# Where the columns of the convolution input and of the gates are computed: whole at the seams, or a few products at a time inside scans and inverses

## The chip, the core and the metric

The kernel runs on one core of a Trainium2 chip. The metric is the device time of one execution in microseconds. The kernel before takes 3205.15 us, the median of three runs (3204.31 to 3208.82).

## What is computed

A decoder trunk of two layers over 528 tokens (16 learned ones put ahead of 512) of width 1024. A layer is a half-step SwiGLU feed-forward, a mixer of two parallel branches, and a second half-step feed-forward; after each comes a layer norm of the sum with what went in. The mixer, cut to what matters here:

```python
z = x @ w_in
glu_a, glu_b, zr, gate_c, gate_r = split(z)          # 1024, 1024, 3328, 1024, 1024 columns
u  = glu_a * sigmoid(glu_b)
yc = silu(layer_norm(conv31(u) + conv_b)) @ conv_wo  # causal, 31 taps, a filter for each channel
yr = rwkv7(zr) @ rwkv_wo                             # 16 heads of 64, a recurrence over the tokens
h  = sigmoid(gate_c) * yc + sigmoid(gate_r) * yr
out = h @ w_out
```

The recurrence keeps a 64 x 64 state S for each head, and each token does `S = S*w + (S @ -kk) (kk*a) + v k`, then `y = S @ r`.

## The kernel before

Everything is float32 in and out. Channels lie on the 128 partitions, tokens along the free axis. A large product is made of three: each operand is split into a high and a low part of a faster 32-bit format (`split`, `wunit`: ACT copies the high part of a weight block, DVE subtracts it from the raw block to get the low one), and high x high, high x low and low x high are added up in PSUM. A **column** is a block of 128 output channels of `x @ w_in`: 8 blocks of 128 input channels x 3 parts x 2 halves of the tokens (264 each) = 48 matmuls of one line (`mac`, L214). Its weights, 512 KB, come by one DMA from SP's queue (L117), and `w_raw` has two buffers. Its result is a PSUM tile `mm`, of which there are two; ACT or DVE reads it out.

The mixer of one layer has these columns: two for the low-rank inputs of the recurrence and one for the first part of the convolution's gate (computed at the mixer's start); three for each of the eight pairs of heads (`prep_pair`: key, receptance, value); and the **31 columns that this change is about**, which stand with one step that needs no column of its own in the list `fill`: `glu_b` and `glu_a` for each of the eight blocks of the convolution's input (after `glu_a` the block's 31 taps can run on DVE, `taps`, L872), then 16 `gate`s. A `gate` column goes through ACT (L884) and a DMA to memory, where the mixer's end fetches it.

The recurrence is done in chunks of 64 tokens, for four **quarters** of four heads each, one after the other. For a quarter q:

- `prep(q)`: six columns and their elementwise work on ACT and DVE.
- `scores(q)`: for each of eight chunks the products of keys and receptances (L1034, L1043), copied by ACT and masked by DVE. They use the one PSUM tile `sc`. Scores of q + 1 are issued in the steps of scan q.
- `substitution(q, g)`: the diagonal 16 x 16 blocks of half g of the chunks are inverted by thirty small DVE instructions; the inverses go through memory into `dd` (L1086, L1089, SP's queue).
- `inverse(q, g)`: for 16 matrices of 64 x 64 at a time, PE joins those blocks: a first round of matmuls (L1112), a mask on DVE (L1113), then three rounds (L1121) with ACT copies (L1125) between them. A fp32 matmul stands as two in the trace.
- `meta(q)`: the 16 learned tokens.
- `scan(q)`: eight **steps**, one for each chunk. In a step PE transposes v (L1183), ACT copies it twice (L1184, L1186), PE multiplies by the state (L1188), ACT copies (L1190), PE applies the inverse (L1196) and reads the state (L1198), ACT copies (L1201), PE updates the state (L1205), DVE adds and scales it (L1208, L1209), and PE finishes the output (L1213), which ACT copies (L1218).
- `post(q)`: a group norm, transposes (L1303), and the result to memory, in the steps of the next scan; for the last quarter in the steps of its own scan and behind it.

The stretch between two scans, with `substitution(q + 1, 1)`, `inverse(q + 1, 0)`, `meta(q + 1)` and `prep(q + 2)`, is called a **seam** below. `inverse(q, 1)` is issued behind step 0 of scan q.

The order of the instructions on each engine is made when the program is built: a planner walks through time by a model of the instructions' durations, and on each engine takes the ready instruction that stands earliest in the program. So program order is priority: work that stands later is drawn forward to where an engine would wait, as far as its inputs and buffers allow. On the chip each engine runs its queue strictly in that order. `high_priority(offset=-n)` makes scores (50) and taps (150) stand later than they are written.

Where columns of `fill` stand in the program is a table of counts: `START` and `LOWSTEP` in the low-rank part, `FILL0` for the chunks of the first scores, `FILLP` inside `prep`, `FILL` behind the steps of each scan, `FILLS` at the seams, and `LAST`, the number kept for the very end, behind the transposes of the last group norm (`self.later = self.turned`). The call is always for whole columns: `filler(n)` pops n entries and each computes all of its 48 products at that place. Before, 8 entries go in the low-rank part, 4 in the first scores, 2 in `prep(1)`, 3 at the first seam, 1 in `prep(2)`, 3 at the second seam, 4 at the third, 3 behind steps of scan 3, 2 after it, then the rest.

## Time and profile before

| | |
|---|---|
| median of three runs | 3205.15 us (3204.31 to 3208.82) |
| the profiled execution: its time, its span | 3213.03 us, 3211.3 us |
| mean granted TensorE clock in it | 0.971 |
| PE, DVE, ACT busy | 3129.7, 1893.0, 1224.3 us |
| HBM read and written | 270.81 MB, 47.12 MB |

The span lies within the profiled execution's own time; the profiled execution was a little longer than the timed runs. "PE" is TensorE's matmuls and "PEld" its weight loads; a matmul's duration includes the depth of the pipeline, so successive matmuls overlap in the record and the starts tell the rate. In a timeline a row is a start, the time from the first start to the last end of a merged group, engine, line, operation, what is written and read, and how many; what follows in brackets is idle time before it and who ended it. In windows a row is a stretch, its length, busy time and count of each engine, the granted clock, the share of the DMA engines and GB/s. The four scans of layer 0 lie between 622 and 1050 us of the span, those of layer 1 between 2232 and 2643.

### The profile page before, as it was taken

What the parts mean: (1) busy time and instruction counts of PE and PEld (TensorE: products, weight loads), DVE (VectorE), ACT (ScalarE), POOL (GpSimd) and SP (SyncE); (2) the same over time, 40 slices, a digit from 0 to 9 for tenths busy, and PEclk for the clock granted to TensorE, in tenths of its full rate; (3) what the DMA queues carried; (4) which work ended last, traced back from release to release, by engine and by line L of the source; (5) the groups of instructions that cost most, each with busy time, mean ns of one, the idle gap of its engine ahead of it and who ended that gap; (6) DMA issues with size and microseconds to landing.
All of it is one profiled execution on the core that took longest, in us unless ns stands there. A gap on an engine that the chain in (4) does not pass through costs nothing.

```text
span 3211.3 us, 64489 instructions
## 1 busy us (share of the span) xinstructions
PE 3129.7 (97%) x27172; PEld 3006.6 (94%) x27172; DVE 1893.0 (59%) x3827; ACT 1224.3 (38%) x2271; POOL 24.0 (1%) x95
## 2 busy tenths in 40 slices
PE   9999999999999899999999999899999999999998
PEld 8999989988889899999989999899899889999997
DVE  4343377886786766343463434777887758653435
ACT  4232254343454534232242322543444445242322
POOL 0000000000000000000000000000000000000000
PEclk9999999997999999999999999998999999999998
DMA  5232244332333552232232322343333325432321
GB/s 153 74 109 83 76 137 149 93 81 77 92 104 92 172 150 80 79 108 81 79 96 74 111 80 81 130 143 91 82 92 104 107 82 179 119 106 77 115 72 54
DMA packets 569776, 326.45 MB, mean 102 GB/s; under 512 B 84940, under 2 KB 536896, under 8 KB 569486
## 3 DMA queue, kind: packets, MB, share of 16 engines
q1 hardware_dynamic: 563374, 308.49, 33.6%
q10 hardware_dynamic: 4608, 8.52, 0.7%
q0 software_dynamic: 1504, 5.33, 0.5%
q8 instruction: 213, 3.49, 0.4%
q14 instruction: 77, 0.63, 0.1%
HBM read 270.81 MB, written 47.12 MB: 99 GB/s over the span
## 4 chain that ended last, share of the span: by engine, by line
PE 89%; DVE 5%; ACT 3%; DMA 2%; issue 1%; SPq 0%; ACTq 0%; POOL 0%; POOLq 0%; DVEq 0%
PE mm L196 54%; PE mm L214 19%; PE sc L1121 3%; PE sc L1043 1%; PE tr L1188 1%; PE ch L1213 1%; PE tr L1196 1%; PE ch L1205 1%; PE sc L1112 1%; PE sc L928 1%; PE sc L797 1%; PE tr L1183 1%; DVE w_lo L139 1%; DVE ln_rstd L390 1%; PE sc L1034 1%
## 5 line engine op out<-in xcount | busy, mean ns | idle before, releaser
L196 PE MATMUL mm<-xh,w_hi 128*128 128x264 f32 (+1 forms) x2880 | 818.9, 285 | 17.6 <-ACT xh L404 16.6
L196 PE MATMUL mm<-xh,w_lo 128*128 128x264 f32 (+1 forms) x2880 | 820.2, 285 | 0.5 <-DVE w_lo L139 0.5
L196 PE MATMUL mm<-xl,w_hi 128*128 128x264 f32 (+1 forms) x2880 | 818.1, 284 | 0.3 <-DVE xl L405 0.2
L139 DVE TENSOR_TENSOR w_lo<-w_raw,w_hi 128x1024 fp32r<-128x1024 f32 (+3 forms) x520 | 528.7, 1017 | 438.8 <-ACT w_hi L128 418.9
L128 ACT CAST w_hi<-w_raw 128x1024 fp32r<-128x1024 f32 (+2 forms) x400 | 385.3, 964 | 765.7 <-PE mm L196 522.0
L196 PEld LDWEIGHTS mm<-xh,w_hi 128*128 128x128 f32 x2880 | 545.1, 190 | 20.7 <-ACT xh L404 18.2
L196 PEld LDWEIGHTS mm<-xh,w_lo 128*128 128x128 f32 x2880 | 546.3, 190 | 0.8 <-DVE w_lo L139 0.8
L196 PEld LDWEIGHTS mm<-xl,w_hi 128*128 128x128 f32 x2880 | 545.6, 189 | 1.4 <-DVE xl L405 1.3
L196 PE MATMUL mm<-hl,w_hi 128*128 128x264 f32 (+1 forms) x1408 | 400.5, 284 | 0.0
L196 PE MATMUL mm<-hh,w_hi 128*128 128x264 f32 (+1 forms) x1408 | 400.4, 284 | 0.0
L196 PE MATMUL mm<-hh,w_lo 128*128 128x264 f32 (+1 forms) x1408 | 398.7, 283 | 0.0
L214 PE MATMUL mm<-xh,w_hi 128*128 128x264 f32 x1760 | 393.6, 300 | 1.7 <-DVE tmp L747 1.7
L214 PE MATMUL mm<-xh,w_lo 128*128 128x264 f32 x1760 | 392.4, 299 | 0.3 <-DVE w_lo L139 0.3
L214 PE MATMUL mm<-xl,w_hi 128*128 128x264 f32 x1760 | 386.4, 297 | 0.0
L872 DVE SCALAR_TENSOR_TENSOR cacc<-cu,cw,cacc 128x528 f32<-128x528 f32 (+1 forms) x480 | 355.1, 751 | 5.9 <-ACT cacc L870 2.7
L214 PEld LDWEIGHTS mm<-xh,w_hi 128*128 128x128 f32 x1760 | 287.6, 195 | 9.2 <-DVE tmp L747 2.2
L214 PEld LDWEIGHTS mm<-xh,w_lo 128*128 128x128 f32 x1760 | 286.6, 195 | 7.3 <-DVE w_lo L139 0.7
L214 PEld LDWEIGHTS mm<-xl,w_hi 128*128 128x128 f32 x1760 | 285.5, 195 | 6.3
L452 DVE TENSOR_TENSOR g<-g,mm 128x264 f32<-128x264 f32 (+1 forms) x176 | 74.6, 427 | 329.3 <-PE mm L196 318.5
L196 PEld LDWEIGHTS mm<-hh,w_lo 128*128 128x128 f32 x1408 | 265.1, 188 | 0.1
L196 PEld LDWEIGHTS mm<-hl,w_hi 128*128 128x128 f32 x1408 | 265.0, 188 | 0.2
L196 PEld LDWEIGHTS mm<-hh,w_hi 128*128 128x128 f32 x1408 | 264.6, 188 | 0.1
(312 smaller groups left out, 4381.3 us busy)
## 6 DMA issues: line engine op xcount, KB each, us to landing
w_raw<-in_w_in_dram SPq DMA_DIRECT2D x116, 512.0 KB
w_raw<-in_ffn_wg_dram SPq DMA_DIRECT2D x88, 512.0 KB
w_raw<-in_ffn_wu_dram SPq DMA_DIRECT2D x88, 512.0 KB
w_raw<-in_ffn_wd_dram SPq DMA_DIRECT2D x64, 384.0 KB
w_raw<-in_ffn_wd_dram SPq DMA_DIRECT2D x64, 320.0 KB
w_raw<-in_rwkv_wo_dram SPq DMA_DIRECT2D x16, 512.0 KB
w_raw<-in_conv_wo_dram SPq DMA_DIRECT2D x16, 512.0 KB
w_raw<-in_w_out_dram SPq DMA_DIRECT2D x16, 512.0 KB
```

The costliest lines, as they stand in the source:

```text
L128: copy = self.nc.scalar.copy(hi[:, :kt], raw[:, :kt])
L139: sub = self.nc.vector.tensor_tensor(lo[:, k], raw[:, k], hi[:, k].bitcast(F32), op=ALU.subtract)
L196: self.nc.tensor.matmul(pm, a[:, k, :], b[:, xk + k, s], start=first and k == 0 and j == 0, stop=last and k == nk - 1 and j == 2)
L214: m = nc.tensor.matmul(pm[:, h, :n], a[:, wk + k, :], b[:, xk + k, s:s + n], start=first and k == 0 and j == 0, stop=last and k == nk - 1 ...
L390: nc.vector.reciprocal(rstd[:, :n], rstd[:, :n])
L452: nc.vector.tensor_tensor(g, g, ps[1][:, :n], op=ALU.mult)
L797: nc.tensor.matmul(pm, w[a][r, o, :], x[b][r, s], start=j == 0, stop=j == 2)
L872: tap = nc.vector.scalar_tensor_tensor(y, x, w, y, op0=ALU.mult, op1=ALU.add)
L928: nc.tensor.matmul(tr[:, 32 * j:32 * j + 32], sq[:, k0:k0 + P], self.bones[:, ::4], start=True, stop=True)
L1034: nc.tensor.transpose(ps[:, 0, 256 + p * P:256 + (p + 1) * P], FB[p][:, fs], self.ident)
L1043: pairs.append(nc.tensor.matmul(ps[:, e, p * P:(p + 1) * P], FB[p][r, fs], G[r, p, 1, :, cs], start=True, stop=True))
L1121: nc.tensor.matmul(ps[0:W, i, c0:C], vt[:, i, :], x[:, c0:C], start=True, stop=True)
```

## The change

`mac` becomes a generator, `macs`, that issues one product at a time. A new function, `pump(n)`, issues up to n products of the column that is open; when none is open it takes the next entry of `fill`, as long as a **quota** for this part of the program lasts, loads its weights if they aren't loaded, and orders the next entry's weights too if the quota goes on. A column's read-out follows its last product. `pump()` without a number finishes the open column and opens none.

A step of a scan calls it at four places: behind the copies of v, 4 products; behind the copy L1190, 5; behind the copy L1201, 4; at the end of the step's products, 7. An inverse calls it with 2 behind every fourth matrix, in the first round and in each of the three others. The quotas are 1 column for `inverse(0, 0)`, 4, 4, 4 and 3 for the four scans with the `inverse(q, 1)` in them, and 1 for each later `inverse(q + 1, 0)`. At the end of a scan the open column is finished and what is left of the quota is computed as whole columns.

The tables `FILL`, `FILLS` and `FILLP` are gone, so no whole columns of `fill` stand at the seams, in `prep` or behind steps; the first scores have 3 instead of 4, and `LAST` is 2 instead of 1. What the columns compute, their number and their order in `fill` stay.

```diff
-FILL0 = (0, 0, 0, 0, 2, 0, 0, 0, 2)
-FILL = ((0, 0, 0, 0, 0, 0, 0, 0), (0, 0, 0, 0, 0, 0, 0, 0), (0, 0, 0, 0, 0, 0, 0, 0), (0, 1, 0, 1, 0, 1, 0, 0))
-FILLS = (3, 3, 4, 2)
-FILLP = ((0, 0, 0, 0, 0, 0), (0, 0, 0, 0, 0, 2), (0, 0, 0, 0, 0, 1), (0, 0, 0, 0, 0, 0))
-LAST = 1
+FILL0 = (0, 0, 0, 0, 1, 0, 0, 0, 2)
+QUOTA0 = 1
+QUOTA = (4, 4, 4, 3)
+QUOTAI = (1, 1, 1)
+PUMP = (4, 5, 4, 7)
+PUMPI = 2
+LAST = 2
...
+    def macs(self, pm, w, x, t0, n, nk):
...
+                    yield m
...
         def prep(q):
             Q = {}
-            for i, _ in enumerate(self.prep(q, Q)):
-                filler(FILLP[q][i])
+            for _ in self.prep(q, Q):
                 self.taps(TAPP[q])
...
         self.substitution(0, 1, Q)
+        self.quota = QUOTA0
         self.inverse(0, 0, Q)
+        self.pump()
         self.meta(0, Q)
...
+            self.quota = QUOTA[q]
             for c, _ in enumerate(self.scan(q, Q)):
...
-                filler(FILL[q][c])
                 self.taps(TAP[q][c])
+            self.pump()
+            filler(self.quota)
             for _ in post:
                 pass
             if q < 3:
                 self.substitution(q + 1, 1, N)
+                self.quota = QUOTAI[q]
                 self.inverse(q + 1, 0, N)
+                self.pump()
                 self.meta(q + 1, N)
             post = early or self.post(q, Q)
-            filler(FILLS[q])
             Q, N = N, prep(q + 2) if q < 2 else None
...
+    def pump(self, n=None):
+
+
+        while n is None or n > 0:
+            if self.open is None:
+                if n is None or not self.quota or not self.fill:
+                    return
+                self.quota -= 1
+                col, done = self.fill.pop(0)
+                w = self.loaded.pop(col) if col in self.loaded else self.load_in(col)
+                if self.quota and self.fill:
+                    nxt = self.fill[0][0]
+                    self.loaded[nxt] = self.load_in(nxt)
+                pm = self.mm()
+                self.open = self.macs(pm, w, self.x, 0, T // 2, KT), done, pm
+            gen, done, pm = self.open
+            if next(gen, None) is None:
+                done(pm)
+                self.open = None
+            elif n is not None:
+                n -= 1
...
         for i in range(N):
             nc.tensor.matmul(ps[0:C, i, 0:W], U[:, i, :], d[:, i, 0:W], start=True, stop=True)
+            if i % 4 == 3:
+                self.pump(PUMPI)
...
                 nc.tensor.matmul(ps[0:W, i, c0:C], vt[:, i, :], x[:, c0:C],
                                  start=True, stop=True)
+                if i % 4 == 3:
+                    self.pump(PUMPI)
...
             nc.scalar.copy(va[0:C], hc(tr[0:C, 0:256]))
+            self.pump(PUMP[0])
...
             nc.scalar.copy(w[0:C], hc(tr[0:C, 256:512]))
+            self.pump(PUMP[1])
...
             nc.scalar.copy(va[C:P], hc(tr[C:P, 256:512]))
+            self.pump(PUMP[2])
...
+            self.pump(PUMP[3])
             ro = C * (c % 2)
```

More of the change, by code (lines that the diff above doesn't have):

```diff
@@ L212, in mac @@
                 for h in range(2):
-                    s = t0 + h * n
-                    m = nc.tensor.matmul(
-                        pm[:, h, :n], a[:, wk + k, :], b[:, xk + k, s:s + n],
-                        start=first and k == 0 and j == 0,
-                        stop=last and k == nk - 1 and j == 2)
+                    m = self.nc.tensor.matmul(
+                        pm[:, h, :n], a[:, k, :], b[:, k, t0 + h * n:t0 + (h + 1) * n],
+                        start=k == 0 and j == 0, stop=k == nk - 1 and j == 2)
                     if self.later is not None:
@@ L274, in setup @@
         self.first = None
+        self.later = None
     def fetch_x(self, h, room):
```

32 lines of the change are left out of this document (16 added, 16 removed).

## The prediction

> **What bounds the kernel now.** I read the page first: the shares by engine, then the chain that ended last.
>
> ```profile
> span 3211.3 us, 64489 instructions
> PE 3129.7 (97%) x27172; PEld 3006.6 (94%) x27172; DVE 1893.0 (59%) x3827; ACT 1224.3 (38%) x2271; POOL 24.0 (1%) x95
> PE 89%; DVE 5%; ACT 3%; DMA 2%; issue 1%; SPq 0%; ACTq 0%; POOL 0%; POOLq 0%; DVEq 0%
> ```
>
> TensorE bounds it: busy for 97% of the span and 89% of the chain. But a busy PE need not be a PE at full rate, so the second view is the windows, by stretch: the whole of each layer's mixer, beside 200 us of a feed-forward layer, and the same mixers for the column products alone (L214, the line this change hands out differently).
>
> ```profile
> 200.00:400.00 200.00, 200.00 (x1644) 199.83 (x1643) 74.58 (x119) 53.02 (x87) 0.00 (x0) 1.00 0.30 87
> 436.00:1072.00 636.00, 621.62 (x5921) 567.71 (x5922) 485.61 (x1166) 287.03 (x598) 8.57 (x36) 0.94 0.39 110
> 2036.00:2665.00 629.00, 615.32 (x5878) 563.25 (x5877) 471.57 (x1098) 286.35 (x593) 8.92 (x39) 0.95 0.39 112
> 436.00:1072.00 636.00, 384.34 (x2640) 345.13 (x2640) 0.94 0.39 110
> ```
>
> Columns here: stretch, its length, then busy time and count of PE, PEld, DVE, ACT, POOL (of PE and PEld alone in the last row), the granted clock, DMA share, GB/s. In the feed-forward a matmul starts every 200/1644 = 0.122 us at clock 1.00. A mixer has 2640 column products, 55 columns of 48, worth 321 us at that rate; its other 3281 matmuls, all smaller, and its waits fill the other half. And the mean clock is 0.94 and 0.95. Where it falls, it falls to 0.50, so (1 - 0.94) x 2 x 636 + (1 - 0.95) x 2 x 629 = 76 + 63 = 139 us of the mixers run at half clock. So what can be gained is in the scans and inverses: waits, and half-clock time. The total of the products is the same before and after.
>
> **The scans' steps.** Four windows that hold exactly six steps each (48 L1188 matmuls, eight a step), with the products in them:
>
> ```profile
> 662.00:698.00 36.00, 13.88 (x67) 9.62 (x68) 1.00 0.20 50
> 2273.00:2307.00 34.00, 12.18 (x58) 8.28 (x58) 1.00 0.21 52
> 2397.00:2437.00 40.00, 16.26 (x83) 11.51 (x83) 1.00 0.37 102
> 2515.00:2553.00 38.00, 14.33 (x68) 9.77 (x68) 1.00 0.36 98
> ...
> 662.00:698.00 36.00, 4.07 (x48) 3.24 (x48) 1.00 0.20 50
> 2515.00:2553.00 38.00, 4.03 (x48) 3.25 (x48) 1.00 0.36 98
> ```
>
> 148 us for 24 steps is 6.17 us a step, with 276/24 = 11.5 products in it already: columns of the seams are drawn into the steps today. The clock is 1.00. What a step costs without them is read off the starts in the timeline of PE, behind one row of the groups by line:
>
> ```profile
> L1196 PE MATMUL tr<-w,G 64*64 64x64 f32 x512 | 46.0, 232 | 0.5 <-ACT w L1190 0.5
> ...
> 689.63 0.68 PE L1205 MATMUL ch<-va,sb 128*64 128x64 f32 x8
> 690.25 0.41 PE L1183 MATMUL tr<-ident,v 128*64 128x128 f32 x2
> 690.58 0.71 PE L1043 MATMUL sc<-G,FB 64*128 64x128 f32 x8
> 691.23 0.68 PE L1213 MATMUL ch<-va,sb 128*64 128x64 f32 x8
> 691.84 0.39 PE L214 MATMUL mm<-xh,w_hi 128*128 128x264 f32 x1
> 692.06 0.41 PE L214 MATMUL mm<-xl,w_hi 128*128 128x264 f32 x2
> 692.31 0.29 PE L214 MATMUL mm<-xh,w_lo 128*128 128x264 f32 x1
> 692.52 0.68 PE L1188 MATMUL tr<-sv,G 128*64 128x64 f32 x8
> 693.13 0.39 PE L214 MATMUL mm<-xh,w_lo 128*128 128x264 f32 x1
> ```
>
> From start to next start L1205 and L1183 take 0.62 and 0.33 us, the scores' L1043 0.65, L1213 and L1188 0.61 each. L1196 runs side by side with L1198; its 46.0 us in 64 steps are 0.72 a step with the last one's tail, against 0.68 for the rows of eight here, so I take 0.61 for it too. The scores' two transposes I put at 0.2, from L1183's two at 0.33 less the change of shape. Together 3.63 us. The 11.5 products add 1.40. Another price shows: the last product before L1188 holds PE for 0.21 us where 0.122 is its rate. Going over to another weight shape costs 0.09, and about as much on the way back (inside the 0.61), so a run of products costs 0.2 us beside its length; four ways in add 0.36 a step. That leaves 6.17 - 3.63 - 1.40 - 0.36 = 0.78 us of true wait per step.
>
> After the change a step hands out 4 + 5 + 4 + 7 = 20 products, each group right behind a stage whose copy the chain waits for. With no wait left a step takes 3.63 + 20 x 0.122 + 0.36 = 6.43 us; with the waits as they are, 7.2. The 8.5 further products are worth 1.04 us elsewhere. So a step gains between 0 and 0.78 us; I take half of the wait as filled, 0.4 us. 24 steps of scans 0 to 2 and 112/20 = 5.6 of scan 3 are fed, 59 in both layers: **-24 us** (0 to -46). DVE hides the work that comes with it:
>
> ```profile
> 662.00:698.00 36.00, 35.97 (x408) 29.37 (x407) 30.48 (x57) 18.80 (x54) 0.00 (x0) 1.00 0.20 50
> L139 DVE TENSOR_TENSOR w_lo<-w_raw,w_hi 128x512 fp32r<-128x512 f32 x120 | 81.8, 682 | 14.1 <-ACT w_hi L126 9.1 <-PE mm L214 3.6 <-ACT w L1190 0.4
> ```
>
> DVE is at 30.48/36 = 85%. A column brings two L139 of 0.68 us: 8.5/48 of it a step is 0.24 us, on 5.1 us of DVE in a step of 6.8. It fits, since the convolution's taps give way. If it did not, L1208 would start late and the step lose that 0.24 us, 14 us in all. The weight loads are the same number, moved from the seams into SP's queue between the scores' stores; DMA is at 0.20 to 0.37 there, and each column is loaded one column ahead, so I cost that at nothing.
>
> The Trainium skill, page "TensorEngine Tiling (Array Packing)", section "Key Properties", says that changing the tiling mode, not just the tile, drains the TensorE; it speaks against short runs of products. The trace shows such a cost, 0.09 us a way, and by the rule it is paid at every switch. It changes a term of mine only where a switch is new, which is the next part.
>
> **The inverses.** The chain of waits at a seam shows how one runs today:
>
> ```profile
> 716.84 2.03 PE sc L1112 x32
> 718.88 4.15 PE mm L214 x20
> 723.03 1.56 PE sc L1121 x32
> 725.14 0.80 PE mm L214 x5
> 725.94 1.55 PE sc L1121 x32
> 728.56 0.80 PE mm L214 x5
> 730.65 2.69 PE sc L1121 x32
> ```
>
> Already 30 products lie in its waits, in three runs. The change puts two behind every four matrices, 16 places. I expect the first round's four places to be new runs and most later products to be drawn into the waits as now: four new pairs, 0.8 us, for 16 inverses 13 us; in the half that lies within a scan the PE changes shape anyway, so **+10 us** (+3 for one pair each to +42 for thirteen).
>
> The same rows show the half clock: 20 products took 4.15 us, 0.2 each, and the last round 2.69 us against 1.55. One inverse had almost no products to fill it (layer 0, scan 1):
>
> ```profile
> 772.00:806.00 34.00, 31.30 (x315) 26.50 (x314) 21.75 (x52) 14.21 (x36) 0.15 (x2) 0.65 0.14 41
> 772.00:806.00 34.00, 4.58 (x21) 3.09 (x20) 0.65 0.14 41
> ```
>
> 21 products in 34 us, and 0.35 x 2 x 34 = 24 us at half clock. The change hands out 32 in that inverse and 20 in each of its four steps, 112. The 91 more are worth 11 us; half of them in waits is **-6 us**. Of the 139 us at half clock I let a third go, 46 us; PE-bound work takes twice as long there, so at most 23 us, and with PE waiting part of it, **-14 us** (+10 if the seams lose as much as the inverses win; -50 if most of it goes).
>
> **What is left bare.** Two places lose their cover. At the seam before scan 3 no preparation of a next quarter follows. Today, in the 14 us from the end of scan 2 to the inverse:
>
> ```profile
> 962.00:976.00 14.00, 13.09 (x100) 12.39 (x100) 1.00 0.56 137
> 971.29 3.90 SPq L1089 DMA_DIRECT2D dd<-xdscr  x8
> ```
>
> 100 products fill the time until the diagonal blocks land (L1089). Afterwards the quota there is one column: 48. 52 x 0.122 = 6.3 us a layer lie idle, less some 1 us because longer steps of scan 2 let the blocks come in earlier: **+11 us** for both (0 to +16). The last group norm:
>
> ```profile
> 2646.55 0.41 PE L214 MATMUL mm<-xh,w_lo 128*128 128x264 f32 x2
> 2650.67 0.41 PE L1303 MATMUL tr<-ident,b 128*128 128x128 f32 x2 [3.71 <-DVE b L1262]
> ...
> 2658.28 0.40 PE L214 MATMUL mm<-xh,w_lo 128*128 128x264 f32 x2
> 2662.58 1.01 PE L196 MATMUL mm<-rh,w_hi 128*128 128x256 f32 x3 [3.89 <-ACT rh L103]
> ```
>
> Today one column is kept for behind the norm's transposes and PE idles 3.71 us before and 3.89 us after it. Keeping two fills the second gap, but nothing is left for before: the norm's 7 us lie bare, and the clock will be down when the two columns start. **+3 us** for both (-4 to +8).
>
> **The sum**: -24 + 10 - 6 - 14 + 11 + 3 = -20 us, made against the profiled execution's 3213.0 us (1.7 us around the span). That execution is 7.9 us above the median of the three times, 3205.15, and I carry the difference over: **3185 us**, 0.6% faster. A difference under 0.2%, 6.4 us, can't be told from none.
>
> **The rivals.** *Filled already* (3205): the steps hold 11.5 products today, and if the 0.8 us is the chain's own latency on ACT and DVE that more products only push back, each step lengthens by what it takes in, the switches take back what the clock gives, and -20 shrinks to within 6 us. For it: the window with 83 products took 40 us and that with 58 took 34; 6 us for 25 products is 0.24 each, twice the rate, if nothing else differs (scores and transposes do).
>
> *Bare seams* (3229, slower): the columns are used up in the steps and PE waits at the seams. If the prepared columns don't cover seams 0 and 1 either, because their evictions wait on DVE behind the substitution, then three columns less there leave some 8 us bare at each, 32 us in both layers; with the steps at half my gain that makes -20 + 32 + 12 = +24. It decides once more than 5 us are idle at each of the four. For it: DVE at 85%; against it: at those seams six columns of preparation, 35 us of products, stand behind.
>
> The Trainium skill, page "TensorE: Matmul & The Clock Gate", section "HAM oscillation", puts the clock at half after an idle stretch beyond some 3.4 us and so works for this rival. In the rows above, 20 products at half clock lost 20 x 0.08 = 1.6 us; at the four places in two layers that is 13 us more, 3242. The trace agrees with the two states only; its half-clock times begin behind runs of small matmuls too, where PE is busy.
>
> *All waits filled* (3140): the steps at their 6.43 us give -46, two thirds of the half clock go, -30, and the inverses' switches stay at +3; with the other terms as above, -65.
>
> *Not as it says*: if the products are drawn to where PE would wait anyway, whatever their place in the program, before and after are one order; that is *filled already* again.
>
> **The chances**: forecast 0.45 (its own range 3165 to 3198), all waits filled 0.15, filled already 0.14, bare seams 0.26. So faster 0.60, same 0.14, slower 0.26. The range leaves out half of each far case: 3125 to 3230.
>
> **What would show it.** In the windows of six steps: some 20 products a step and a period of 6.8 us; 6.2 would be *all waits filled*, 7.2 and more *filled already*. The mixers' granted clock: 0.96 or more. The window 772 to 806's counterpart at clock 1.00. In the 14 us before L1112 of scan 3: 48 products and an idle gap of 5 us. Before the last L1303 an idle gap near 7 us, and none before L196. The prediction is wrong in its core if the mixers' other waits grow by what the steps save, or if L1208 starts later behind DVE's L139.

## The result, and the profile after

The change makes the kernel **slower**: 3256.47 us (median of four runs, 3248.24 to 3259.88) against 3206.99 for the kernel before on the same chip, a ratio of 1.0155 with a 95% interval of 1.0135 to 1.0175. The prediction had said 3185, 3125 to 3230: wrong in sign, and outside its range. The profiled execution's span is 3252.9 us, 41.6 above that of before.

The head of the page after:

```profile
span 3252.9 us, 64508 instructions
PE 3156.6 (97%) x27172; PEld 3022.1 (93%) x27172; DVE 1899.4 (58%) x3831; ACT 1221.9 (38%) x2275; POOL 23.9 (1%) x95
PE 89%; DVE 5%; DMA 2%; ACT 2%; issue 1%; ACTq 0%; SPq 0%; DVEq 0%
```

The same 27172 matmuls, and PE is still 97% busy and 89% of the chain. The page alone doesn't show where 42 us went: PE's busy time grew by 27 of them, for the same number of matmuls. The windows of the two whole mixers show one reason:

```profile
437.00:1095.00 658.00, 638.05 (x5912) 578.30 (x5912) 486.71 (x1165) 283.92 (x595) 8.29 (x34) 0.92 0.37 107
2065.00:2703.00 638.00, 616.93 (x5841) 559.24 (x5841) 471.61 (x1096) 281.41 (x589) 8.08 (x33) 0.94 0.39 109
```

The clock went down, from 0.94 and 0.95 to 0.92 and 0.94. By the prediction's own sum that is 0.08 x 2 x 658 + 0.06 x 2 x 638 = 182 us at half clock where it was 139 (rounding of the clock leaves some 7 us to each mixer).

The next view finds the place. The mixer of layer 0 is cut between the same instructions in both kernels: up to the end of the preparation at the second seam; scan 2; the seam before scan 3 up to the end of its inverse; scan 3; and from there to the first matmul of the mixer's end. Each row is one stretch for the column products alone: its length, busy time and number of products on PE and PEld, the clock, the share of DMA, GB/s. First the kernel before (L214):

```profile
436.70:909.70 473.00, 302.61 (x2131) 277.41 (x2131) 0.94 0.39 111
909.70:960.00 50.30, 18.18 (x95) 13.07 (x95) 1.00 0.35 96
960.00:991.90 31.90, 20.35 (x141) 18.69 (x141) 0.90 0.48 127
991.90:1050.00 58.10, 28.80 (x159) 21.96 (x159) 0.94 0.26 74
1050.00:1069.90 19.90, 14.40 (x114) 14.00 (x114) 0.94 0.59 185
```

and the changed one (L218):

```profile
437.50:911.20 473.70, 319.12 (x2188) 286.67 (x2188) 0.95 0.40 114
911.20:975.20 64.00, 30.94 (x163) 22.65 (x163) 1.00 0.30 84
975.20:1004.90 29.70, 11.99 (x75) 10.20 (x75) 0.75 0.45 117
1004.90:1070.40 65.50, 20.73 (x118) 16.66 (x118) 0.76 0.22 62
1070.40:1095.80 25.40, 13.71 (x96) 13.57 (x96) 0.77 0.43 142
```

Up to scan 2 nothing is lost: 57 more products are done in the same time. All of the loss stands from scan 2 on, in 184.6 us instead of 160.2, although 57 products fewer are done there. In layer 1 it is the same in two rows a kernel, up to scan 2 and from there on, before and after:

```profile
2040.00:2503.00 463.00, 308.72 (x2142) 280.94 (x2143) 0.95 0.40 113
2503.00:2662.60 159.60, 82.71 (x498) 67.78 (x498) 0.95 0.38 109
```

```profile
2065.20:2525.20 460.00, 317.04 (x2195) 284.76 (x2195) 0.97 0.41 117
2525.20:2703.00 177.80, 75.76 (x445) 61.96 (x445) 0.87 0.32 91
```

The **scans' steps**: two windows after that hold exactly six steps each, as those of before in the prediction; the first for all engines, then the products of both. Between the product rows stands the counterpart of the window of layer 0, scan 1, in which before had its pocket with only 21 products.

```profile
660.00:700.00 40.00, 40.00 (x468) 34.09 (x465) 33.31 (x68) 19.69 (x54) 0.00 (x0) 1.00 0.20 53
...
660.00:700.00 40.00, 18.77 (x98) 13.56 (x99) 1.00 0.20 53
776.00:810.00 34.00, 16.48 (x93) 12.37 (x92) 1.00 0.30 87
2543.00:2586.00 43.00, 19.98 (x103) 14.54 (x103) 1.00 0.30 81
```

The steps take in 98/6 = 16 and 103/6 = 17 products. Against the windows of before (67 products in 36 us, 68 in 38) that is 31 products for 4 us and 35 for 5, 0.13 and 0.14 us each: no less than the 0.122 that a product takes in the feed-forward. The windows are a rough measure, since the first holds 29 other matmuls more than its counterpart before (a whole round of an inverse among them) and the second 45 fewer. The whole of scan 2 in layer 0 is a better one: it has 513 other matmuls in both kernels, and by the rows above 68 more products made it 13.7 us longer, 0.20 each. PE is recorded busy for 40.00 of 40.00 us, and it had been for 35.97 of 36: no wait is seen that could be filled. The pocket is another matter: 93 products instead of 21 in the same 34 us, the clock at 1.00 instead of 0.65.

The **inverse** within scan 2, by the chain of work: before,

```profile
913.18 1.99 PE sc L1112 x32
915.17 0.49 PE tr L1188 x6
915.66 1.17 PE mm L214 x8
916.83 1.43 PE sc L1121 x29
...
918.74 0.68 PE mm L214 x4
919.42 1.57 PE sc L1121 x32
921.00 0.61 PE ch L1205 x8
...
922.43 1.55 PE sc L1121 x32
```

and after:

```profile
914.37 1.99 PE sc L1142 x32
916.36 1.92 PE mm L218 x14
918.28 1.56 PE sc L1153 x32
919.84 1.64 PE mm L218 x12
921.49 1.55 PE sc L1153 x32
923.04 0.44 PE mm L218 x2
...
924.04 1.55 PE sc L1153 x32
```

The places "behind every fourth matrix" don't show in the trace: the rounds stand whole, and the planner puts the products into the waits between them, as it did before. What changed is what else stood there. Before, the products shared these waits with the step's own matmuls (L1188, L1196, L1198, L1205, L1183), so that a step ran inside the inverse. After, the products stand ahead of that step in program order, 28 of them take the waits, and the step comes behind the inverse.

**Scan 3** is where the quota is used up. In layer 0 its last product runs at 1041.4 us, right behind the last round of the inverse within it (the chain has it as)

```profile
1041.40 0.32 PE mm L218
```

and the steps after it have none. The products in the last three steps of layer 0 before:

```profile
1033.20:1050.00 16.80, 9.01 (x49) 6.65 (x49) 1.00 0.31 92
```

and after, all engines and then products:

```profile
1049.30:1070.40 21.10, 16.89 (x132) 12.44 (x130) 7.87 (x25) 7.48 (x19) 1.25 (x2) 0.50 0.15 48
...
1049.30:1070.40 21.10, 0.00 (x0) 0.00 (x0) 0.50 0.15 48
```

Three steps with 49 products take 16.8 us; with none they take 21.1, at half clock throughout. And behind them the waits of PE after, from 960 to 1100 us (engine, tile and line, for whom; total, number, longest):

```profile
PE tr L1341 <- DVE b L1300: 6.8, 1, 6.8
PE mm L198 <- ACT rh L105: 3.9, 1, 3.9
```

Before the last norm's transposes (L1341) PE idles for 6.8 us. Before, it was 3.7 in layer 1, by the prediction's rows, and in layer 0, by the same view,

```profile
PE tr L1303 <- DVE b L1262: 0.4, 1, 0.4
```

since products filled it. The two columns kept for behind the norm then run with nothing beside them, 96 products.

### The profile page after: what moved, and what is told of

Same layout as the page of the kernel before. It is cut to its first block, busy times and chain, and to the rows that moved or that the text cites. A ratio compares the mean times of both kernels' runs of the same rounds, so it can differ in the third digit from the quotient of the medians.

```text
span 3252.9 us, 64508 instructions
## 1 busy us (share of the span) xinstructions
PE 3156.6 (97%) x27172; PEld 3022.1 (93%) x27172; DVE 1899.4 (58%) x3831; ACT 1221.9 (38%) x2275; POOL 23.9 (1%) x95
## 4 chain that ended last, share of the span: by engine, by line
PE 89%; DVE 5%; DMA 2%; ACT 2%; issue 1%; ACTq 0%; SPq 0%; DVEq 0%
PE mm L198 53%; PE mm L218 20%; PE sc L1153 3%; PE sc L1073 2%; PE tr L1223 1%; PE ch L1250 1%; PE tr L1232 1%; PE ch L1242 1%; PE sc L1142 1%; DVE w_lo L141 1%; DMA w_raw<-in_ffn_wg_dram 1%; PE sc L832 1%; PE tr L1217 1%; PE sc L958 1%; DVE ln_rstd L395 1%
## 5 line engine op out<-in xcount | busy, mean ns | idle before, releaser
L198 PE MATMUL mm<-xh,w_hi 128*128 128x264 f32 (+1 forms) x2880 | 821.2, 286 | 17.7 <-ACT xh L409 17.0
L198 PE MATMUL mm<-xh,w_lo 128*128 128x264 f32 (+1 forms) x2880 | 822.4, 286 | 0.5 <-DVE w_lo L141 0.5
L198 PE MATMUL mm<-xl,w_hi 128*128 128x264 f32 (+1 forms) x2880 | 820.5, 285 | 0.3 <-DVE xl L410 0.2
L198 PEld LDWEIGHTS mm<-xh,w_hi 128*128 128x128 f32 x2880 | 547.2, 190 | 20.5 <-ACT xh L409 18.6
L198 PEld LDWEIGHTS mm<-xh,w_lo 128*128 128x128 f32 x2880 | 548.4, 190 | 0.8 <-DVE w_lo L141 0.8
L198 PEld LDWEIGHTS mm<-xl,w_hi 128*128 128x128 f32 x2880 | 548.1, 190 | 0.9 <-DVE xl L410 0.9
L198 PE MATMUL mm<-hl,w_hi 128*128 128x264 f32 (+1 forms) x1408 | 401.0, 285 | 0.0
L198 PE MATMUL mm<-hh,w_hi 128*128 128x264 f32 (+1 forms) x1408 | 400.9, 285 | 0.0
L198 PE MATMUL mm<-hh,w_lo 128*128 128x264 f32 (+1 forms) x1408 | 399.3, 284 | 0.0
L218 PE MATMUL mm<-xh,w_hi 128*128 128x264 f32 x1760 | 393.8, 301 | 3.0 <-DVE tmp L782 1.7
L218 PE MATMUL mm<-xh,w_lo 128*128 128x264 f32 x1760 | 393.0, 300 | 1.7 <-DVE w_lo L141 1.7
L218 PE MATMUL mm<-xl,w_hi 128*128 128x264 f32 x1760 | 391.4, 299 | 0.0
L218 PEld LDWEIGHTS mm<-xh,w_hi 128*128 128x128 f32 x1760 | 286.2, 195 | 11.2 <-DVE tmp L782 2.2
L218 PEld LDWEIGHTS mm<-xh,w_lo 128*128 128x128 f32 x1760 | 285.7, 195 | 10.6 <-DVE w_lo L141 2.7
L218 PEld LDWEIGHTS mm<-xl,w_hi 128*128 128x128 f32 x1760 | 285.9, 195 | 8.4 <-issue 0.2
L198 PEld LDWEIGHTS mm<-hh,w_lo 128*128 128x128 f32 x1408 | 265.5, 189 | 0.1
L198 PEld LDWEIGHTS mm<-hl,w_hi 128*128 128x128 f32 x1408 | 265.3, 188 | 0.2
L198 PEld LDWEIGHTS mm<-hh,w_hi 128*128 128x128 f32 x1408 | 264.9, 188 | 0.1
```

The source lines that it names most:

```text
L198: self.nc.tensor.matmul(pm, a[:, k, :], b[:, xk + k, s], start=first and k == 0 and j == 0, stop=last and k == nk - 1 and j == 2)
L218: m = self.nc.tensor.matmul(pm[:, h, :n], a[:, k, :], b[:, k, t0 + h * n:t0 + (h + 1) * n], start=k == 0 and j == 0, stop=k == nk - 1 and ...
```

## The experiments

Each kernel ran beside the kernel before on the same chip; the ratios are to that one, with 95% intervals, and gains are told as differences of these ratios (0.1% is 3.2 us; the change loses 1.55%, 50 us). The first theory was about **the clock and the empty steps** (A in the expectations), the second about **order** (C: the products stand ahead of the chain's own matmuls; D, its rival, blames the changes of weight shape), and the third, to which misses of the second led, about **supply** (scan 2 takes in columns that scan 3 and the end then lack).

### Empty steps

`fed3` hands out the products of scan 3 in smaller numbers, to spread them over all of its steps.

```diff
-PUMP = (4, 5, 4, 7)
+PUMPS = ((4, 5, 4, 7), (4, 5, 4, 7), (4, 5, 4, 7), (2, 2, 2, 3))
...
-            self.pump(PUMP[0])
+            self.pump(PUMPS[q][0])
```

> The changed kernel, but scan 3 hands out 2, 2, 2 and 3 products at its four places instead of 4, 5, 4 and 7, so that its three columns last for all eight steps and some 40 products are left behind the last step. Theory A (the loss sits behind the used-up quota: steps 4 to 7 of scan 3 without products fall to half clock): those steps go from 7.4 us back to about 6.2 at clock 1.00, the bare group norm is half covered and the last two columns start at full clock; 8 to 14 us a layer, so 3256 becomes 3228 to 3240. Theory B (the steps are paced by their chain of copies, and the runs of a few products only lengthen them, at any clock): the same products are in the same scan, 3250 to 3262.

3250.70 us, 1.0147 (1.0118 to 1.0176). Scan 3 holds the same 118 and 114 products as in the change: the planner had drawn them forward all the same, so the kernel didn't do what it was to test. It tells nothing about the steps, but it shows that handing products out in smaller numbers, a little further back in the program, doesn't hold them back.

`dummy` is the change with 96 products more a layer that nobody reads: 12 in each of the steps 4 to 7 of scan 3, and 48 behind the last.

```diff
+            if q == 3 and c > 3:
+                self.idle_products(3)
```

> The changed kernel with work added and none moved: in steps 4 to 7 of scan 3 three products whose result nobody reads stand at each of the four places, and 48 more behind the last step, 96 a layer or 11.7 us of PE time at the full rate. Theory A (half clock): although there is more to do, steps 4 to 7 get shorter, 7.4 to some 6.5 us, and the last two columns take 11.8 us instead of 17.6; 3256 becomes 3236 to 3250. Theory B (waits, not the clock): the added products cost what they take where PE isn't waiting, 3258 to 3275.

3242.76 us, 1.0124 (1.0106 to 1.0142): 10 us faster than the change by the ratios (14 by the times), with 192 products more. The same three steps in its windows:

```profile
1049.30:1065.90 16.60, 16.60 (x182) 14.24 (x181) 6.26 (x16) 6.91 (x18) 0.70 (x1) 1.00 0.30 93
```

16.6 us at clock 1.00 instead of 21.1 at 0.50. Scan 3 fell from 65.5 and 64.1 us in the two layers to 61.7 and 57.7. So the empty steps lose by the clock, and products that nobody reads win this part back, some 10 us of the 50. The end didn't gain (25.5 and 26.4 us).

### Order

`noinv` takes the pieces out of the inverses; the seam's column stands whole behind the inverse.

```diff
-PUMPI = 2
+PUMPI = 0
...
                 self.inverse(q + 1, 0, N)
                 self.pump()
+                filler(self.quota)
```

> The changed kernel without products inside the inverses: the same quotas, but the seams' column is computed whole behind the inverse, and scans hand theirs out in the steps alone. If the new changes of weight shape in the inverses cost what the prediction put on them (10 us) this gives 3246; if they were drawn into the waits anyway and keep the clock up there, 3256 to 3270. It also feeds the steps of scan 3 with 32 more products, which by theory A is worth 3 us a layer, and by theory B nothing.

3233.96 us, 1.0094 (1.0075 to 1.0112): 20 us of the 50 come back, more than in either case of the expectation. So the 10 us that the prediction put on the inverses don't explain it.

`whole` has the same quotas with no pieces at all: whole columns behind every second step.

```diff
-QUOTA = (4, 4, 4, 3)
+QUOTA = (0, 0, 0, 0)
+FILL = ((0, 1, 0, 1, 0, 1, 0, 1),) * 3 + ((0, 1, 0, 1, 0, 1, 0, 0),)
-PUMP = (4, 5, 4, 7)
-PUMPI = 2
+PUMP = (0, 0, 0, 0)
+PUMPI = 0
```

> The changed kernel with the same number of columns for each scan and seam, but every column whole: one behind every second step, one behind each seam's inverse, none inside steps or inverses. Theory A (the loss comes from where the columns are, not from how they are cut): 3246 to 3262, as slow as the change. Theory B (it comes from handing out a few at a time): back to the kernel before, 3200 to 3225.

3219.82 us, 1.0044 (1.0021 to 1.0067): 36 us come back.

`late200` and `late600` keep every piece where the change puts it, and make it stand 200 or 600 places later for the planner.

```diff
+LATE = 200
...
-            if next(gen, None) is None:
+            with self.tc.high_priority(offset=-LATE):
+                left = next(gen, None)
+            if left is None:
```

> The changed kernel, same quotas and same places, but the handed-out products (not their weights) stand 200 places later in the planner's order than they are written, so behind the next steps' own work. Theory C (the products stand ahead of the chain: the planner fills the waits of an inverse and of a step with them first, and the scan's own next matmuls wait behind them): the inverses inside scans hold one to two steps again as in the kernel before, steps 3 to 7 take what before's took; scans 0 to 2 lose nothing any more, scan 3 and the tail stay bare: 3212 to 3232. Theory D (the runs of a few products and their changes of weight shape cost it): 3248 to 3262.

> As the 200, with 600 places. Theory C: products are then pure filling for waits, and some of them slide to the seams and behind scan 3, where they are missing: 3200 to 3225, not slower than with 200. Theory D: 3248 to 3262.

3210.84 us, 1.0012 (1.0000 to 1.0025), and 3208.73, 1.0005 (0.9994 to 1.0016): 46 and 48 us come back. With 600, scan 2 holds 117 and 119 products instead of 163 and 156, and scan 3 136 and 144 instead of 118 and 114. So late pieces also shift the supply; this pair alone can't tell order from supply.

`stepend` has no pieces in the inverses, and all 20 of a step at its end.

```diff
-PUMP = (4, 5, 4, 7)
-PUMPI = 2
+PUMP = (0, 0, 0, 20)
+PUMPI = 0
```

> The changed kernel with no products inside inverses and each step's 20 in one place, at its end, instead of four places inside the step. Against the kernel without inverse products (3234): theory C says that a product behind the step's own matmuls doesn't hold this step up, only the next one's first: 3220 to 3234. Theory D, with fewer runs, says the same direction but less in the inverses; if it is the same 3234 within 4, the place inside the step does not matter.

3244.01 us, 1.0112 (1.0096 to 1.0129), where 3220 to 3234 was expected: a miss. It is 6 us above `noinv`, hardly clear of the intervals, so the places inside a step are not what costs.

`whole_tail` is `whole` with two columns fewer in scan 2 and one column, not two, behind the last norm.

```diff
-FILL = ((0, 1, 0, 1, 0, 1, 0, 1),) * 3 + ((0, 1, 0, 1, 0, 1, 0, 0),)
+FILL = ((0, 1, 0, 1, 0, 1, 0, 1),) * 2 + ((0, 0, 0, 1, 0, 0, 0, 1), (0, 1, 0, 1, 0, 1, 0, 0))
-LAST = 2
+LAST = 1
```

> Whole columns as in the run with whole columns (3220), but scan 2 gets two instead of four, so that seven are left for scan 3 and the end as in the kernel before, and one instead of two stays behind the last transposes. Theory A for what is left (steps 4 to 7 of scan 3 bare, at half clock): scan 3 and the tail return to 58 and 20 us a layer; the run with whole columns was some 8 us a layer ahead at the start of scan 2, so 3185 to 3203, faster than both. If the end of the mixer isn't what costs, 3212 to 3222.

3198.85 us, 0.9976 (0.9965 to 0.9987): faster than both kernels. The 22 us against `whole` come from two numbers that have nothing to do with pieces.

### Supply

`tail_only` therefore does only that to the change; every piece stays where and how it was.

```diff
-QUOTA = (4, 4, 4, 3)
+QUOTA = (4, 4, 2, 3)
-LAST = 2
+LAST = 1
```

> The change with the last quotas alone altered: scan 2 has two columns instead of four, and LAST is 1, so three columns stand behind scan 3 before the last group norm and one behind it. If the end is a loss of its own (the stretch behind scan 3 took 25.4 and 25.8 us against 19.8 and 20.0 before, and scan 2 took in 163 products against 95), some 5 us a layer at the end and a few in scan 2 come back: 3237 to 3248. If the end is only where a loss made earlier shows, the time stays within 3252 to 3258.

3209.28 us, 1.0014 (0.9993 to 1.0035): 45 us of the 50 come back, where 8 to 19 were expected. Its windows from scan 2 on, products of layer 0, and in the last row the products in the last three steps of scan 3:

```profile
906.20:960.20 54.00, 20.18 (x113) 15.19 (x113) 1.00 0.30 85
960.20:990.60 30.40, 18.50 (x132) 17.01 (x132) 0.90 0.48 130
990.60:1051.70 61.10, 27.81 (x159) 21.87 (x159) 0.94 0.29 85
1051.70:1071.10 19.40, 7.78 (x48) 7.64 (x48) 0.71 0.39 139
...
1035.80:1051.70 15.90, 3.92 (x20) 2.81 (x20) 1.00 0.42 128
```

The same 452 products as in the change (163 + 75 + 118 + 96) take 164.9 us instead of 184.6. Scan 2 gives up 50 and is 10 us shorter, the seam has 57 more at about the same length, and in the last three steps, with twenty products, the clock is 1.00. PE still idles 6.8 us ahead of the last norm's transposes here: the three columns that stand ahead of it were drawn forward into the seam and scan 3, and it is there that they pay.

`late_tail` has both remedies: `late600` with the quotas of `tail_only`.

> The products as pieces at the places of the change, 600 places later in the planner's order, and the quotas of the kernel before this one in the list (two columns in scan 2, three columns behind scan 3, LAST 1). If order and end are two losses that add up, the end gives some 8 to 12 us beside the 3208.7 of the same pieces without it: 3196 to 3202, about what whole columns with that end took (3198.9). If pieces, once they stand late, fill the waits better than whole columns do, under 3195. If late pieces had already filled the end's waits, 3206 to 3210.

3203.98 us, 0.9989 (0.9972 to 1.0006). The two don't add: 45 and 48 us apart, 53 together.

`late_inv` and `late_steps` make only the pieces of the inverses, or only those of the steps, 600 places later (the edit is against `late600`; the second has the two numbers exchanged).

```diff
-LATE = 600
+LATE = 0
+LATEI = 600
...
-            with self.tc.high_priority(offset=-LATE):
+            with self.tc.high_priority(offset=-late):
...
-                self.pump(PUMPI)
+                self.pump(PUMPI, LATEI)
```

> The change with the products that an inverse calls for 600 places later; those of the steps stay where the change puts them. Leaving the inverses' pieces out gave 3234 of 3256. If that was the chain of rounds that waited behind them, standing late gives the same, 3230 to 3238; if it was the switches of shape or the number of places, which stay, 3250 or more.

> The change with the products that a step calls for 600 places later; those of the inverses stay where the change puts them. All products late gave 3208.7 of 3256.5, and the inverses' share was 22 by leaving theirs out. If the two shares add up, the steps' share is about 26: 3227 to 3235. If the step's own waits lose nothing to products ahead of them (they were to be filled), 3250 or more.

3262.05 us, 1.0171 (1.0141 to 1.0201), and 3223.14, 1.0052 (1.0032 to 1.0071). The first is a clear miss for order: nothing is won. Its scans 2 hold 165 products each, and its scans 3 only 78 and 91, fewer than in any kernel here. Supply says that such a kernel is slow, order that it is fast. Supply doesn't explain all of it: up to scan 2 it takes 947 us in both layers together, 13 more than the change. Its expectation put 3250 or more down to the changes of weight shape; `noinv_tail` below bears on that. The second won 33 us, a little more than its 3227 to 3235.

Four kernels to tell the two apart. `two_behind` and `last_one` are `tail_only` split into its two numbers: the first gives scan 2 two columns instead of four, the second keeps one behind the last norm instead of two.

> The change with two columns instead of four in scan 2 and nothing else; the two are left for the place behind scan 3, ahead of the last group norm, and two stay behind it. Supply theory: scan 2 falls from 64 to about 54 us a layer, scan 3 draws the two columns forward and gains 4 us or so, the end stays at 25 us: 3218 to 3230. Order theory (the products that stay are still ahead of the chain): 3240 to 3256.

> The change with one column instead of two behind the last group norm and nothing else; scan 2 keeps four. Supply theory: the end falls from 25.5 to 20 us a layer and scan 3 draws one column forward, so 10 to 16 us in all come back: 3238 to 3247. If the two numbers do nothing apart and all together, 3250 or more.

3228.69 us, 1.0071 (1.0046 to 1.0095), and 3229.69, 1.0070 (1.0046 to 1.0094): 27 us each, where both together gave 45. In `two_behind` scan 2 falls from 64.0 and 62.3 to 54.1 and 52.9 us, and the end stays at 25.4 and 25.9; in `last_one` scan 2 stays at 64.0 and 62.3, scan 3 falls from 65.5 and 64.1 to 59.7 and 55.7, the end to 18.9 and 19.4. `last_one` came out better than its expectation, since scan 3 gained more from one column than was put down.

`noinv_tail` is `noinv` with the quotas of `tail_only`.

> The supply of the 3209 us kernel (two columns in scan 2, three ahead of the last norm, one behind it) without pieces in the inverses, whose columns stand whole behind them. If the inverses' pieces cost 22 us whatever the supply, 3185 to 3192. If leaving them out gave those 22 us only because it left more for scan 3, 3203 to 3213.

3205.47 us, 0.9999 (0.9984 to 1.0014): the inverses' pieces, with their places and any changes of weight shape, cost 5 us here, not 20, and by the intervals perhaps nothing. In `noinv` scan 2 had 23 and 24 products fewer than in the change and was 6 and 7 us shorter, while scan 3 gained nothing in sum; so leaving them out had helped there mainly by relieving scan 2.

`before_early` turns it round: the kernel before, with no pieces, and its three columns of scan 3 behind steps of scan 2.

```diff
-FILL = ((0, 0, 0, 0, 0, 0, 0, 0), (0, 0, 0, 0, 0, 0, 0, 0), (0, 0, 0, 0, 0, 0, 0, 0), (0, 1, 0, 1, 0, 1, 0, 0))
+FILL = ((0, 0, 0, 0, 0, 0, 0, 0), (0, 0, 0, 0, 0, 0, 0, 0), (0, 1, 0, 1, 0, 1, 0, 0), (0, 0, 0, 0, 0, 0, 0, 0))
```

> The kernel before, whole columns and no pieces; only the three columns behind steps 1, 3 and 5 of scan 3 stand behind steps 1, 3 and 5 of scan 2 instead. Supply theory: scan 2 takes in some 150 products at 0.19 us each beyond the 95 it took, scan 3 and its end lack them, and the stretch from scan 2 to the end grows from 160 us a layer to 172 to 185: 3230 to 3255, the loss of the change without a single piece. Order theory: whole columns behind the steps cost nothing there, 3203 to 3213.

3218.58 us, 1.0025 (1.0011 to 1.0039), between the two. Scan 2 grew to 61.2 us with 159 products, but the columns of the seam and of the end were drawn forward in their turn, and scan 3 had 259 products. It was full, not starved, and the end stayed at 18.9 us.

`before_starved` does both in the kernel before: nothing is left for scan 3's steps or the place behind it, and two columns are kept for the end.

```diff
-FILL = ((0, 0, 0, 0, 0, 0, 0, 0), (0, 0, 0, 0, 0, 0, 0, 0), (0, 0, 0, 0, 0, 0, 0, 0), (0, 1, 0, 1, 0, 1, 0, 0))
+FILL = ((0, 0, 0, 0, 0, 0, 0, 0), (0, 0, 0, 0, 0, 0, 0, 0), (0, 1, 1, 1, 0, 1, 1, 0), (0, 0, 0, 0, 0, 0, 0, 0))
-FILLS = (3, 3, 4, 2)
+FILLS = (3, 3, 4, 0)
-LAST = 1
+LAST = 2
```

> The kernel before, whole columns and no pieces, with the supply of the change at its end: the three columns behind steps of scan 3 and the two after it stand behind steps 1, 2, 3, 5 and 6 of scan 2, none is left for the place behind scan 3, and two stand behind the last group norm. Supply theory: the end rises from 20 to 25 us a layer, scan 3 has no products in its later steps, scan 2 takes in some 50 to 70 more; the stretch from scan 2 to the end grows from 160 to 175 to 185 us: 3235 to 3257. Order theory (products must stand ahead of the chain in pieces to do harm): 3205 to 3222, as for the kernel that only filled scan 2 (3218.6).

3264.52 us, 1.0178 (1.0150 to 1.0205). The loss of the change, and more, without a single piece; it lies above the 3235 to 3257 expected of supply, and far from the 3205 to 3222 of order. From scan 2 on, products of layer 0, and its last three steps of scan 3:

```profile
910.90:984.90 74.00, 41.49 (x239) 32.22 (x239) 1.00 0.35 97
984.90:1002.20 17.30, 4.90 (x20) 3.48 (x20) 0.75 0.42 109
1002.20:1078.50 76.30, 21.17 (x154) 20.96 (x154) 0.72 0.23 68
1078.50:1103.40 24.90, 13.19 (x96) 13.05 (x96) 0.77 0.43 145
...
1057.90:1078.50 20.60, 16.84 (x132) 12.46 (x131) 9.18 (x40) 7.49 (x19) 1.26 (x2) 0.50 0.14 47
```

The signs are those of the change: scan 2 overfull, the clock at 0.75 at the seam and 0.72 in scan 3, the last three steps 20.6 us at 0.50, the end at 25 us. The supply is broken further than in the change: scan 2 took in 144 products more than before, where 50 to 70 were expected.

`late200_tail` asks once more whether order adds to the right supply: `late200` with the quotas of `tail_only`.

> The supply of the 3209 us kernel (two columns in scan 2, three ahead of the last norm, one behind it) with all pieces 200 places later in the planner's order. The stretch up to scan 2 took 914.5 us in two layers with pieces 200 later (935.9 in the kernel before), the stretch from scan 2 on 318 to 324 with this supply: some 15 us under the kernel before if the two hold together, 3187 to 3195. If order and supply are one loss seen twice, 3200 to 3210, as with 600.

3202.53 us, 0.9983 (0.9970 to 0.9996). The 15 us against the kernel before didn't come; 10 us against `tail_only` did, little more than the intervals allow to be told. The time lies in the range put down for order and supply being one loss seen twice.

The kernels side by side: the median time, and for layer 0 us / products from the trace, cut as above:

| kernel | time, us | scan 2 | seam | scan 3 | end |
|---|---|---|---|---|---|
| before | 3207 | 50.3 / 95 | 31.9 / 141 | 58.1 / 159 | 19.9 / 114 |
| the change | 3256 | 64.0 / 163 | 29.7 / 75 | 65.5 / 118 | 25.4 / 96 |
| late_inv | 3262 | 61.5 / 165 | 27.5 / 121 | 66.2 / 78 | 25.4 / 96 |
| before_starved | 3265 | 74.0 / 239 | 17.3 / 20 | 76.3 / 154 | 24.9 / 96 |
| last_one | 3230 | 64.0 / 163 | 29.8 / 75 | 59.7 / 166 | 18.9 / 48 |
| two_behind | 3229 | 54.1 / 113 | 29.7 / 132 | 66.1 / 111 | 25.4 / 96 |
| tail_only | 3209 | 54.0 / 113 | 30.4 / 132 | 61.1 / 159 | 19.4 / 48 |
| late600 | 3209 | 51.5 / 117 | 29.4 / 129 | 58.5 / 136 | 25.6 / 96 |
| whole_tail | 3199 | 53.8 / 99 | 31.0 / 139 | 54.1 / 154 | 20.7 / 72 |

The number of products alone doesn't set a scan's time: where they lie in it does too (the 154 of `before_starved` all stand in its first 24 us).

**Settled**: the loss is supply, that is, what is left for scan 3 and the end once scan 2 has taken its share. By the rows above the two layers together take 936 us up to scan 2 before and 934 in the change, and 319.8 and 362.4 from there on. Restoring the supply in the change gives back 45 of 50 us with all pieces in place (323.5 us from scan 2 on), and breaking it in the kernel before, further than the change does, makes the loss without pieces.

**Open**: how much order is worth by itself. With the right supply, fewer pieces, later pieces or none won 5 to 12 us (`noinv_tail`, `late_tail`, `late200_tail`, `whole_tail`), and the intervals are some 5 us wide to each side. The stretch up to scan 2 shows where it lies. The six kernels with the change's products there (the change, `fed3`, `dummy`, `tail_only`, `two_behind`, `last_one`) take 931 to 939 us in both layers; `late200`, `late200_tail`, `late600` and `whole` take 914 to 923, with 30 to 58 products fewer, which are worth 4 to 7 us at 0.122. Against the mean of the six, 936, some 6 to 15 us there look like order, by one execution of each; `late_inv`, 13 us longer than the change there, stays unexplained. With 163 products in scan 2 and 96 at the end as in the change, `whole` lost 14 us and not 50: this gain and the 137 products in its scan 3 explain it only in part.

## Why the prediction was wrong, by its own steps

Its terms can be set against the trace of layer 0 if a product is priced at 0.122 us wherever it lies. Up to scan 2: +0.7 - 57 x 0.122 = -6.3. Scan 2: +13.7 - 68 x 0.122 = +5.4. The seam before scan 3: -2.2 + 66 x 0.122 = +5.9. Scan 3: +7.4 + 41 x 0.122 = +12.4. The end: +5.5 + 18 x 0.122 = +7.7. Together +25.1. Layer 1, cut and priced in the same way, has -9.5, +5.0, +1.7, +14.2 and +3.8, together 460.0 + 177.8 - 463.0 - 159.6 = +15.2. In all that is 40 of the 42 us between the spans.

- **The steps, -24: wrong; this is the first step that failed.** "That leaves 0.78 us of true wait per step" was the remainder of a sum of row durations, not a wait: a row quoted there has PE busy for 35.97 of 36 us. Part of the remainder is work that the sum leaves out: each of the four windows holds 16 matmuls of line 1020, and 56 of L1213 where the sum counts 48, by my estimate from their rows some 0.2 us a step; the rest is not accounted for. Added products cost 0.13 and 0.14 us each in the windows and 0.20 in scan 2, so they lengthened the steps and filled nothing there. The rival *filled already* (0.24 a product read from two windows, and "each step lengthens by what it takes in") was right about the steps.
- **What the quota leaves bare in scan 3: missing from the sum; this is the costliest.** "5.6 of scan 3 are fed" was right to say that some steps are not. It let those cost what they did before. They cost 21.1 us for three instead of 16.8, because they had held products before and their clock fell. Scan 3 is +12.4 in layer 0 and +14.2 in layer 1, with no term for it.
- **The seam, +11 for both layers**: 5.9 in layer 0 and 1.7 in layer 1, the right size in the first, but by another way and so by luck. Instead of 48 products and 5 us idle there are 75 and no such gap, but the clock is 0.75 instead of 0.90.
- **The end, +3 for both: too small by a factor of four (7.7 and 3.8).** The 6.8 us ahead of the norm came as foreseen. "Keeping two fills the second gap" was wrong: the 3.9 us ahead of L198 are still there, behind whatever column comes last. So the second column covers neither gap; in `last_one`, which moves it ahead of the norm, the end is 6.5 and 6.4 us shorter.
- **The half clock, -14: wrong in sign.** 182 us instead of 139. "Of the 139 us at half clock I let a third go" has no row behind it but the pocket's. By the clocks in the rows above, the half-clock time of both layers up to scan 2 did go down, from some 105 to 75 us, with 110 products more there; from scan 2 on it rose from some 30 to 105. If work at half clock takes twice as long, these 30 us less are worth 15, about the 16 won up to scan 2 in both layers, and the 75 more cost up to 37 of the 56 lost behind it; this is an estimate.
- **The pocket, -6: right**, if small. 72 products more in the same 34 us are worth 8.8 us in layer 0, and the clock there is 1.00. It lies within the -6.3 up to scan 2, where the idea of the change works.
- **The inverses, +10: wrong in form.** No new runs appear: the sixteen inverses hold 54 runs of products, 55 before. The products take the waits from the step's own matmuls; with supply put right that costs about 5 us, if anything (`noinv_tail`).

The rival *bare seams* had the mechanism ("the columns are used up in the steps and PE waits") and the sign. It looked at seams 0 and 1, where preparation stands behind, and not at scan 3, behind which nothing stands. It put the deciding signal at more than 5 us of idle time of PE at each seam. There is almost none at the seam before scan 3; in scan 3 PE idles 6.7 us in layer 0, in pieces under a microsecond, and the half clock comes on top.

## What to carry to other kernels

Work that only fills waits is a supply: ask of every stretch what it has left after an earlier one has taken more, the last stretch first, since nothing can be drawn into it from behind. Read from a row of busy time whether a wait exists before pricing what fills it, and take the price of an added product from two stretches that hold the same other work; a remainder of a sum of durations is not a wait. A planner that draws work forward will use up what stands ahead, so hold back by count what the end needs: two numbers in a table were worth 45 us here, and with them put right the finely cut work was at best 5 us faster than the kernel before (`late200_tail`).

## What the hardware showed

The clock falls to half while PE is mostly busy. The longest wait of PE after, from 1045 to 1070 us in scan 3 of layer 0, and the last and least busy of five windows of that stretch:

```profile
PE tr L1223 <- ACT va L1220: 1.5, 2, 0.8
```

```profile
1065.00:1070.00 5.00, 3.32 (x31) 2.46 (x31) 0.54 (x2) 1.73 (x5) 0.00 (x0) 0.50 0.08 26
```

No wait is longer than 0.8 us, PE is busy for two thirds of the time and more, and the clock is 0.50 in all five; with 20 products in three steps (`tail_only`) it is 1.00. Waits aren't even needed. At the seam before scan 3, among the small matmuls of the inverse, the clock is 0.50 for 20 us while PE is recorded busy without a break; all engines and then products:

```profile
990.00:1010.00 20.00, 20.00 (x177) 17.96 (x177) 9.43 (x22) 2.97 (x9) 0.00 (x0) 0.50 0.21 62
...
990.00:1010.00 20.00, 5.20 (x17) 3.81 (x17) 0.50 0.21 62
```

So a busy row doesn't tell the clock, and what decides it stays open: 20 products in 15.9 us went with 1.00, 17 in these 20 us with 0.50. The Trainium skill, page "TensorE: Matmul & The Clock Gate", section "HAM oscillation", tells of idle stretches beyond some 3.4 us; none is here, so that rule doesn't explain these rows. The same page's section "A second HAM failure mode: psum-queue depth-cycling" tells of short idles between groups of matmuls that make the clock swing between half and full. The trace agrees in part: short idles and a low clock stand together in scan 3, but there it stays at 0.50 for 25 us, and at the seam no idle is recorded.
